# A two-layer encoder in split float32: two products of the up-projection joined into one 512-column matmul, and some weight splits moved to POOL

## The chip, the core and the metric

The kernel runs on one core of a Trainium2 chip. The core has a matrix engine (TensorE, in the rows PE, with its weight loads as PEld), a vector engine (VectorE, DVE), a scalar engine (ScalarE, ACT), a general engine (GpSimd, POOL) and SyncE (SP), which issues the DMA transfers. Engines take their instructions in order and wait for one another by semaphores. Matmuls write to PSUM, which here is cut into eight banks of 128 x 512 float32; everything else lies in SBUF.

The metric is the device time of one execution in microseconds (us). It was 642.43 us before the change: the median of three runs that lay between 642.16 and 642.54.

## The reference

One sequence of 256 positions with 1024 features goes through two layers. Each layer adds the output of two groups of attention heads, and then a gated feed-forward network (FFN) with a short convolution. The FFN is the part that the change touches:

```python
D_FF = 2816
def conv_ffn(h, w_up, conv_w, conv_b, w_down):        # h: rmsnorm(x), 256 x 1024
    u = h @ w_up                                      # 256 x 5632, gate and up columns
    u = conv1d(u, conv_w, width 3, per column) + conv_b
    g, up = jnp.split(u, 2, axis=-1)
    return (jax.nn.silu(g) * up) @ w_down             # 256 x 1024
for l in range(2):
    x = x + attention_groups(rmsnorm(x), ...) @ w_out
    x = x + conv_ffn(rmsnorm(x, ffn_norm[l]), w_up[l], conv_w[l], conv_b[l], w_down[l])
```

All weights and activations are float32.

## The kernel before

A float32 product is made from three products of a faster matmul type (fp32r). Each operand is split into a high part, which is the operand rounded to that type, and a low part, which is what is left; then hi·hi, hi·lo and lo·hi are added up in PSUM. The fourth, lo·lo, is left out. So every product appears three times in the code and in the rows.

**Weights.** The class Weights (L138 to L225) streams all weights through SBUF in one fixed order of units. Raw tiles of 2048 columns come by DMA (`load`, L158); four may be in flight or in use, and a unit of the FFN has 1024 columns, so that a raw tile holds two. For each unit `split_hi` copies the raw columns on ACT into the high part `wh` (L176), and `split_lo` subtracts on DVE raw minus high into the low part `wl` (L189). Six pairs of `wh` and `wl` exist. `fill` issues the next splits, as many as the units already used up by TensorE allow.

**FFN.** The 2816 columns are cut into NF = 22 blocks of 128. Stage j does three things.

- `up(j)` on PE: the gate half and the up half, each with a weight unit of its own. A half takes 8 steps k over the 1024 features, and each step has three products of 128 x 256 columns: high weights with high x (`xh`, L1106), high weights with low x (`xl`, L1107) and low weights with high x (L1108). From j = 2 on both halves lie side by side in one PSUM bank: the bank A for j = 2, then two banks S in turn. The stages 0 and 1 have a bank for each half and are begun before the rest.
- `gate(j)`: DVE multiplies the bank by `r2b`, the RMS scale of each position (one 128x512 product, L284). ACT makes scale and bias of the convolution's middle tap (two Identity copies, L296), four scalar-times-tensor-plus-tensor instructions on DVE add the other taps (L293), ACT does Silu, DVE multiplies the two halves, ACT copies the result to `mh` (high), and DVE subtracts to get `ml` (low). Three times in `gate` a `W.fill(2)` puts weight splits between these steps.
- `down(j-3)` on PE: the 128 rows of the down weights that belong to the block three stages back. For each of four output tiles it adds `mh`·high, `ml`·high and `mh`·low (L1150 to L1152, 128 x 512 each), 12 products into four banks that stay open for the whole layer.

The last four down blocks are held back to the end of the layer, where they are done tile by tile, so that the next layer's norm can begin early. The up weights come from the same stream as the down weights, in the order gate j, up j, down j-3: in layer 0 the units 30+3j, 31+3j and 32+3j.

The order inside one engine is set in two ways. The attention part and the first halves of the stages 0 and 1 are written in program order. The loop over j (L1172 to L1188) is ordered by the language's scheduler, by its own estimates; so the places where weight splits stand among the gate's steps differ from stage to stage, and a change in the loop can move them.

POOL does small work for the attention, and nothing in the FFN.

Of the kernel before, what the change touches and what calls it, by code (L numbers as in the profile page):

```python
# [11 lines left out]
F32R = mybir.dt.float32r  # L12
I32 = mybir.dt.int32
AF = mybir.ActivationFunctionType
ALU = mybir.AluOpType
# [4 lines left out]
P = 128  # L20
LINE = 32
D_MODEL = 1024
SEQ = 256
# [9 lines left out]
NF = D_FF // P  # L33
# [12 lines left out]
FFN_HOLD = 4  # L46
# [91 lines left out]
class Weights:  # L138
# [41 lines left out]
    def split_lo(self):  # L180
        u = self.n_lo
        t, o, last = self.where[u]
        n = self.units[u][-1]
        hi = self.parts[u][0]
        lo = self.w_pool.tile([P, 1024], F32R, name=f"wl{u}", tag="wlo")
        g = self.gain(self.units[u])
        raw, hi = self.raw[t][:, o:o + n], hi.bitcast(F32)[:, :n]
        if g is None:
            self.nc.vector.tensor_tensor(out=lo[:, :n], in0=raw, in1=hi, op=ALU.subtract)  # L189
        else:  # L190
            self.nc.vector.scalar_tensor_tensor(out=lo[:, :n], in0=raw, scalar=g, in1=hi,
                                                op0=ALU.mult, op1=ALU.subtract)
        self.parts[u].append(lo)
        self.n_lo += 1
        if last:
            del self.raw[t]
            self.load()
# [43 lines left out]
def encoder(ctx: ExitStack, tc: tile.TileContext, wpk, x, prm, cst, oh, rb, pos, out):  # L241
# [4 lines left out]
    work = ctx.enter_context(tc.tile_pool(name="work", bufs=2))  # L246
# [5 lines left out]
    def nm(s):  # L252
        uid[0] += 1
        return f"{s}_{uid[0]}"

    def wide():
        return work.tile([P, 512], F32, name=nm("t2"), tag="t2", bufs=7)

    def mid():
        return work.tile([P, 256], F32, name=nm("t1"), tag="t1", bufs=9)  # L260
# [4 lines left out]
    def small(n, dt=F32):  # L265
        return work.tile([P, max(n, LINE)], dt, name=nm("s"), tag=f"s{n}_{dt}", bufs=8 if n <= 32 else 2)[:, :n]
# [4 lines left out]
    def bank():  # L271
        return psa.tile([P, 512], F32, name=nm("S"), tag="S", bufs=2)

    def tbank():
        return psa.tile([P, 512], F32, name=nm("A"), tag="A", bufs=1)

    def obank():
        return psa.tile([P, 512], F32, name=nm("O"), tag="O", bufs=1)

    def acc():  # L280
        return psa.tile([P, 512], F32, name=nm("acc"), tag="acc", bufs=4)

    def tt(o, a, b, op):
        nc.vector.tensor_tensor(out=o, in0=a, in1=b, op=op)  # L284
# [7 lines left out]
    def stt(o, a, s, b, op0, op1):  # L292
        nc.vector.scalar_tensor_tensor(out=o, in0=a, scalar=s, in1=b, op0=op0, op1=op1)  # L293

    def act(o, a, f, **kw):
        nc.scalar.activation(o, a, f, **kw)  # L296
# [15 lines left out]
    mm = nc.tensor.matmul  # L312
# [143 lines left out]

    def new_xT():
        s = State()
        s.hi = work.tile([P, 8, SEQ], F32R, name=nm("xh"), tag="xh", bufs=1)
        s.lo = work.tile([P, 8, SEQ], F32R, name=nm("xl"), tag="xl", bufs=1)  # L460
        s.ss = small(4)
        return s

# [154 lines left out]
    def layer(l, sx, late, bias):  # L618
# [360 lines left out]
        sf = new_xT()  # L979
# [105 lines left out]
        r2b = work.tile([P, SEQ], F32, name=nm("r2b"), tag="r2b", bufs=1)  # L1085

        def ffn_scale():
            xT_stats(sf)
            ob = obank()
            dg = mid()  # L1090
            for t in range(2):
                ts(dg[:, t * P:t * P + P], ident, sf.r[:, t:t + 1], ALU.mult)
            mm(ob[:, :SEQ], ones, dg, start=True, stop=True)
            act(r2b, ob[:, :SEQ], AF.Copy)
# [4 lines left out]
        def up(j, pu, ks=range(8)):  # L1099
            for half in range(2):  # L1100
                u = u_f + FFN_AT[("gate", "up")[half], j]
                hi, lo = W.get(u)
                o = pu[half][:, :SEQ] if len(pu) == 2 else pu[0][:, half * SEQ:(half + 1) * SEQ]
                for k in ks:
                    kp = slice(k * P, k * P + P)
                    mm(o, hi[:, kp], sf.hi[:, k, :], start=k == 0, stop=False)  # L1106
                    mm(o, hi[:, kp], sf.lo[:, k, :], start=False, stop=False)  # L1107
                    mm(o, lo[:, kp], sf.hi[:, k, :], start=False, stop=k == 7)  # L1108
                if ks[-1] == 7:
                    W.done(u)  # L1110

        def gate(j, pu):
            s, y = wide(), wide()
            if len(pu) == 2:
                for g in range(2):
                    tt(s[:, g * SEQ:(g + 1) * SEQ], pu[g][:, :SEQ], r2b, ALU.mult)
            else:
                tt(s.rearrange("p (g t) -> p g t", g=2), pu[0].rearrange("p (g t) -> p g t", g=2),
                   r2b.unsqueeze(1).to_broadcast([P, 2, SEQ]), ALU.mult)
            for g in range(2):  # L1120
                b = j + NF * g
                act(y[:, g * SEQ:(g + 1) * SEQ], s[:, g * SEQ:(g + 1) * SEQ], AF.Identity,
                    scale=cw[:, 44 + b:45 + b], bias=cb[:, b:b + 1])
            W.fill(2)
            for g in range(2):
                b = j + NF * g
                yg, sg = y[:, g * SEQ:(g + 1) * SEQ], s[:, g * SEQ:(g + 1) * SEQ]
                stt(yg[:, 1:], sg[:, :SEQ - 1], cw[:, b:b + 1], yg[:, 1:], ALU.mult, ALU.add)
                stt(yg[:, :SEQ - 1], sg[:, 1:], cw[:, 88 + b:89 + b], yg[:, :SEQ - 1], ALU.mult, ALU.add)
            sl, gt = mid(), mid()  # L1130
            act(sl, y[:, :SEQ], AF.Silu)
            W.fill(2)
            tt(gt, sl, y[:, SEQ:], ALU.mult)
            m = State()
            m.hi = work.tile([P, 1, SEQ], F32R, name=nm("mh"), tag="mh", bufs=6)
            m.lo = work.tile([P, 1, SEQ], F32R, name=nm("ml"), tag="ml", bufs=6)
            act(m.hi[:, 0, :], gt, AF.Copy)
            W.fill(2)
            tt(m.lo[:, 0, :], gt, m.hi.bitcast(F32)[:, 0, :], ALU.subtract)
            gates[j] = m  # L1140
# [13 lines left out]
        def down(j):  # L1154
            for t in range(2):
                for c in range(2):
                    down_mm(j, t, c)
            W.done(u_f + FFN_AT["down", j])
# [13 lines left out]
        for j in range(NF):  # L1172
            if j < 2:
                pu = first[j]
                up(j, pu, range(4, 8))
            else:
                pu = [tbank() if j == 2 else bank()]
                up(j, pu)
            if j == 0:
                continue  # L1180
            if j == 1:
                ffn_scale()
                gate(0, first[0])
            gate(j, pu)
            if j == 1:
                box["a"] = [[acc(), acc()], [acc(), acc()]]
            if FFN_LAG <= j < NF + FFN_LAG - FFN_HOLD:
                down(j - FFN_LAG)  # L1188
# [101 lines left out]
```

## Time and profile before

| | before |
|---|---|
| median of three runs | 642.43 us |
| the profiled execution | 642.16 us |
| its span (first to last instruction) | 640.4 us |
| PE busy | 627.8 us, 98% |
| DVE busy | 497.4 us, 78% |
| ACT busy | 395.8 us, 62% |
| POOL busy | 58.9 us, 9% |
| TensorE clock granted, mean | 0.996 of full speed |

The profiled execution lies 0.27 us under the median, and 1.76 us of it lie outside the span. Busy time of an engine is the union of its instructions. A duration of an instruction runs from its start to its last write; engines overlap the end of one with the start of the next, so that the distance from start to start (the pitch) is shorter than the duration when instructions stand close. The FFN of layer 0 lies between about 134 and 320 us of the span, that of layer 1 between about 446 us and the end.

### The profile page before, as it was taken

What the parts mean: (1) busy time and instruction counts of PE and PEld (TensorE: products, weight loads), DVE (VectorE), ACT (ScalarE), POOL (GpSimd) and SP (SyncE); (2) the same over time, 40 slices, a digit from 0 to 9 for tenths busy, and PEclk for the clock granted to TensorE, in tenths of its full rate; (3) what the DMA queues carried; (4) which work ended last, traced back from release to release, by engine and by line L of the source; (5) the groups of instructions that cost most, each with busy time, mean ns of one, the idle gap of its engine ahead of it and who ended that gap; (6) DMA issues with size and microseconds to landing.
All of it is one profiled execution on the core that took longest, in us unless ns stands there. A gap on an engine that the chain in (4) does not pass through costs nothing.

```text
span 640.4 us, 10656 instructions
## 1 busy us (share of the span) xinstructions
PE 627.8 (98%) x4018; PEld 554.6 (87%) x4018; DVE 497.4 (78%) x1010; ACT 395.8 (62%) x723; POOL 58.9 (9%) x173
## 2 busy tenths in 40 slices
PE   8999999999999999999999999999999999999997
PEld 7967867789999999999899887677999999999995
DVE  4796779679977777777699867876899777777773
ACT  5982867648655555555478557765685555555541
POOL 3950250000000000000001105200000000000000
PEclk8999999999999999999999999999999999999999
DMA  8759425133665455554336512423337445545401
GB/s 314 267 204 174 180 74 198 67 132 139 209 246 180 171 180 193 198 196 152 106 130 262 192 66 75 151 104 133 141 143 278 172 188 197 198 173 170 152 1 66
DMA packets 17706, 105.18 MB, mean 164 GB/s; under 512 B 2102, under 2 KB 3799, under 8 KB 6648
## 3 DMA queue, kind: packets, MB, share of 16 engines
q1 hardware_dynamic: 17368, 104.17, 46.6%
q8 instruction: 31, 0.51, 0.3%
q10 hardware_dynamic: 288, 0.34, 0.2%
q14 instruction: 19, 0.16, 0.1%
HBM read 103.20 MB, written 1.31 MB: 163 GB/s over the span
## 4 chain that ended last, share of the span: by engine, by line
PE 89%; DVE 5%; POOL 3%; issue 1%; ACT 1%; DMA 1%; SPq 0%; DVEq 0%
PE S L1108 12%; PE S L1107 12%; PE S L1106 12%; PE acc L1152 6%; PE acc L1151 6%; PE acc L1150 6%; PE acc L499 4%; PE acc L497 4%; PE acc L498 4%; PE S L558 3%; PE acc L944 2%; PE O L607 2%; PE acc L947 2%; PE acc L946 2%; PE A L535 1%; POOL s L304 1%
## 5 line engine op out<-in xcount | busy, mean ns | idle before, releaser
L176 ACT ACTIVATE wh<-raw 128x1024 fp32r<-128x1024 f32 (+3 forms) x188 | 193.0, 1036 | 96.4 <-PE S L1107 63.5
L189 DVE TENSOR_TENSOR wl<-raw,wh 128x1024 fp32r<-128x1024 f32 (+3 forms) x188 | 223.1, 1190 | 26.6 <-ACT wh L176 26.3
L1108 PE MATMUL S<-xh,wl 128*128 128x256 f32 x640 | 181.0, 283 | 0.0
L1107 PE MATMUL S<-xl,wh 128*128 128x256 f32 x640 | 181.0, 283 | 0.0
L1106 PE MATMUL S<-xh,wh 128*128 128x256 f32 x640 | 180.8, 283 | 0.0
L1107 PEld LDWEIGHTS S<-xl,wh 128*128 128x128 f32 x640 | 122.7, 192 | 1.4
L1106 PEld LDWEIGHTS S<-xh,wh 128*128 128x128 f32 x640 | 122.6, 192 | 1.6
L1108 PEld LDWEIGHTS S<-xh,wl 128*128 128x128 f32 x640 | 122.7, 192 | 0.0
L293 DVE SCALAR_TENSOR_TENSOR t<-t,prm_s,t 128x255 f32<-128x255 f32 x176 | 73.9, 479 | 1.0 <-ACT t L296 0.9
L1152 PE MATMUL acc<-wl,mh 128*128 128x512 f32 x176 | 69.3, 394 | 0.0
L1150 PE MATMUL acc<-wh,mh 128*128 128x512 f32 x176 | 69.3, 394 | 0.0
L1151 PE MATMUL acc<-wh,ml 128*128 128x512 f32 x176 | 69.2, 393 | 0.0
L497 PE MATMUL acc<-wh,xh 128*128 128x512 f32 (+2 forms) x160 | 61.6, 385 | 1.0 <-ACT nat L296 0.9
L499 PE MATMUL acc<-wl,xh 128*128 128x512 f32 (+2 forms) x160 | 58.6, 366 | 0.2 <-DVE wl L189 0.2
L498 PE MATMUL acc<-wh,xl 128*128 128x512 f32 (+2 forms) x160 | 58.3, 364 | 0.2 <-DVE xl L293 0.2
L296 ACT ACTIVATE t<-t,prm_s 128x256 f32<-128x256 f32 x88 | 47.7, 590 | 6.6 <-DVE t L284 6.6
L296 ACT ACTIVATE mh<-t 128x256 fp32r<-128x256 f32 x44 | 18.2, 415 | 46.4 <-DVE t L284 46.4
L284 DVE TENSOR_TENSOR t<-S,r2b 128x512 f32<-128x512 f32 (+1 forms) x42 | 27.9, 665 | 23.0 <-PE S L1108 22.9
L296 ACT ACTIVATE t<-A 96x256 f32<-96x256 f32 (+2 forms) x40 | 18.8, 469 | 43.8 <-PE A L535 26.6
L1152 PEld LDWEIGHTS acc<-wl,mh 128*128 128x128 f32 x176 | 33.1, 188 | 7.5
L1150 PEld LDWEIGHTS acc<-wh,mh 128*128 128x128 f32 x176 | 33.4, 190 | 5.9
L1151 PEld LDWEIGHTS acc<-wh,ml 128*128 128x128 f32 x176 | 33.1, 188 | 6.1
(173 smaller groups left out, 965.0 us busy)
## 6 DMA issues: line engine op xcount, KB each, us to landing
raw<-in_wpk_dram SPq DMA_DIRECT2D x86, 1024.0 KB, 4.8
raw<-in_wpk_dram SPq DMA_DIRECT2D x3, 896.0 KB, 4.4
raw<-in_wpk_dram SPq DMA_DIRECT2D x3, 768.0 KB, 5.6
raw<-in_wpk_dram SPq DMA_DIRECT2D x2, 816.0 KB, 5.2
Bn<-scr SPq DMA_DIRECT2D x8, 192.0 KB, 10.7
raw<-in_wpk_dram SPq DMA_DIRECT2D x2, 720.0 KB, 5.6
X<-in_x_dram SPq DMA_DIRECT2D x3, 256.0 KB, 4.8
raw<-in_wpk_dram SPq DMA_DIRECT2D x2, 384.0 KB, 5.1
```

Of the source, the lines that this page charges most:

```text
L176: self.nc.scalar.activation(hi[:, :n], self.raw[t][:, o:o + n], AF.Copy, scale=1.0 if g is None else g)
L189: self.nc.vector.tensor_tensor(out=lo[:, :n], in0=raw, in1=hi, op=ALU.subtract)
L296: nc.scalar.activation(o, a, f, **kw)
L497: mm(o, lhs.hi[:, k, sl], rh, start=k == 0, stop=False)
L498: mm(o, lhs.lo[:, k, sl], rh, start=False, stop=False)
L499: mm(o, lhs.hi[:, k, sl], rl, start=False, stop=k == ktot - 1)
L1106: mm(o, hi[:, kp], sf.hi[:, k, :], start=k == 0, stop=False)
L1107: mm(o, hi[:, kp], sf.lo[:, k, :], start=False, stop=False)
L1108: mm(o, lo[:, kp], sf.hi[:, k, :], start=False, stop=k == 7)
L1150: mm(o, m.hi[:, 0, sl], hi[:, cs], start=j == 0, stop=False)
L1151: mm(o, m.lo[:, 0, sl], hi[:, cs], start=False, stop=False)
L1152: mm(o, m.hi[:, 0, sl], lo[:, cs], start=False, stop=j == NF - 1)
```

## The change

From stage 2 on, `up` multiplies the high weights with the high and the low x in one matmul of 512 columns. For that, `xh` and `xl` become two halves of one tile (`xhl`). The first 256 columns of the result hold hi·hi and the other 256 hold hi·lo; the product lo·hi still has 256 columns and adds to the first. Since a half now fills a whole bank, each half has a bank of its own: even stages use the banks A and O, odd stages two banks S.

The two column groups must be added before the gate's first step. ACT copies the second group of each half from PSUM to a tile `c`, DVE adds the first group from PSUM and `c`, and the product with `r2b` then has both operands in SBUF.

The low splits of down weights of the blocks 0 to 14 go from DVE to POOL, 15 in each layer. Stages 0 and 1 are computed as before.

```diff
--- before.py
+++ after.py
@@ -186,7 +186,9 @@
         g = self.gain(self.units[u])
         raw, hi = self.raw[t][:, o:o + n], hi.bitcast(F32)[:, :n]
         if g is None:
-            self.nc.vector.tensor_tensor(out=lo[:, :n], in0=raw, in1=hi, op=ALU.subtract)
+            down = self.units[u][1] == "down" and self.units[u][2][0] < NF - FFN_HOLD - 3
+            eng = self.nc.gpsimd if down else self.nc.vector
+            eng.tensor_tensor(out=lo[:, :n], in0=raw, in1=hi, op=ALU.subtract)
         else:
             self.nc.vector.scalar_tensor_tensor(out=lo[:, :n], in0=raw, scalar=g, in1=hi,
                                                 op0=ALU.mult, op1=ALU.subtract)
@@ -456,8 +458,8 @@
 
     def new_xT():
         s = State()
-        s.hi = work.tile([P, 8, SEQ], F32R, name=nm("xh"), tag="xh", bufs=1)
-        s.lo = work.tile([P, 8, SEQ], F32R, name=nm("xl"), tag="xl", bufs=1)
+        s.both = work.tile([P, 2, 8, SEQ], F32R, name=nm("xhl"), tag="xhl", bufs=1)
+        s.hi, s.lo = s.both[:, 0], s.both[:, 1]
         s.ss = small(4)
         return s
 
@@ -1100,22 +1102,31 @@
             for half in range(2):
                 u = u_f + FFN_AT[("gate", "up")[half], j]
                 hi, lo = W.get(u)
-                o = pu[half][:, :SEQ] if len(pu) == 2 else pu[0][:, half * SEQ:(half + 1) * SEQ]
+                o = pu[half]
                 for k in ks:
                     kp = slice(k * P, k * P + P)
-                    mm(o, hi[:, kp], sf.hi[:, k, :], start=k == 0, stop=False)
-                    mm(o, hi[:, kp], sf.lo[:, k, :], start=False, stop=False)
-                    mm(o, lo[:, kp], sf.hi[:, k, :], start=False, stop=k == 7)
+                    if j < 2:
+                        mm(o[:, :SEQ], hi[:, kp], sf.hi[:, k, :], start=k == 0, stop=False)
+                        mm(o[:, :SEQ], hi[:, kp], sf.lo[:, k, :], start=False, stop=False)
+                        mm(o[:, :SEQ], lo[:, kp], sf.hi[:, k, :], start=False, stop=k == 7)
+                        continue
+                    mm(o.rearrange("p (g t) -> p g t", g=2), hi[:, kp], sf.both[:, :, k, :], start=k == 0, stop=False)
+                    mm(o[:, :SEQ], lo[:, kp], sf.hi[:, k, :], start=False, stop=k == 7)
                 if ks[-1] == 7:
                     W.done(u)
 
         def gate(j, pu):
-            s, y = wide(), wide()
-            if len(pu) == 2:
-                for g in range(2):
-                    tt(s[:, g * SEQ:(g + 1) * SEQ], pu[g][:, :SEQ], r2b, ALU.mult)
-            else:
-                tt(s.rearrange("p (g t) -> p g t", g=2), pu[0].rearrange("p (g t) -> p g t", g=2),
+            s, y, c = wide(), wide(), wide() if j >= 2 else None
+            for g in range(2):
+                sg, pg = s[:, g * SEQ:(g + 1) * SEQ], pu[g][:, :SEQ]
+                if j < 2:
+                    tt(sg, pg, r2b, ALU.mult)
+                    continue
+                cg = c[:, g * SEQ:(g + 1) * SEQ]
+                act(cg, pu[g][:, SEQ:], AF.Copy)
+                tt(sg, pg, cg, ALU.add)
+            if j >= 2:
+                tt(s.rearrange("p (g t) -> p g t", g=2), s.rearrange("p (g t) -> p g t", g=2),
                    r2b.unsqueeze(1).to_broadcast([P, 2, SEQ]), ALU.mult)
             for g in range(2):
                 b = j + NF * g
@@ -1174,7 +1185,7 @@
                 pu = first[j]
                 up(j, pu, range(4, 8))
             else:
-                pu = [tbank() if j == 2 else bank()]
+                pu = [bank(), bank()] if j % 2 else [tbank(), obank()]
                 up(j, pu)
             if j == 0:
                 continue
```

In `NF - FFN_HOLD - 3` NF is 22 and FFN_HOLD is 4. `tbank` and `obank` give the banks A and O, `bank` gives the next S, `wide` a 128 x 512 tile of SBUF out of a pool of seven, `act` an ACT instruction and `tt` a two-operand DVE instruction. In the changed kernel L284 becomes L286, L293 becomes L295, L296 becomes L298, and the line of the low split, L189, becomes L191.

The order on TensorE inside a half (`S` is the bank, `wh` and `wl` are high and low weights, `xh` and `xl` the two parts of x) was, for each k:

```order
L1106 MATMUL S_2443<-xh_896,wh_2328 128x256
L1107 MATMUL S_2443<-xl_897,wh_2328 128x256
L1108 MATMUL S_2443<-xh_896,wl_2405 128x256
```

and is now, at the end of one half and the start of the next:

```order
L1113 MATMUL S_2225<-xhl_895,wh_2113 128x512
L1114 MATMUL S_2225<-xhl_895,wl_2187 128x256
L1113 MATMUL S_2226<-xhl_895,wh_2185 128x512
```

Two rows stand where three stood, and the second half goes to another bank.

On DVE, in the middle of an FFN, a stage of before (`t2` are the gate's wide tiles, `t1` its narrow ones, `wl` the low splits, and `x4` means four instructions alike):

```order
L189 TENSOR_TENSOR wl90_3615<-raw47_3354,wh90_3536 128x1024
L284 TENSOR_TENSOR t2_562_3514<-S_561_3465,r2b_406_1783 128x512
L189 TENSOR_TENSOR wl91_3619<-raw47_3354,wh91_3613 128x1024
L293 SCALAR_TENSOR_TENSOR t2_563_3515<-t2_562_3514,prm_s_74,t2_563_3515 128x255 x4
L189 TENSOR_TENSOR wl92_3632<-raw48_3435,wh92_3617 128x1024
L284 TENSOR_TENSOR t1_565_3534<-t1_564_3533,t2_563_3515 128x256
L284 TENSOR_TENSOR ml_567_3544<-t1_565_3534,mh_566_3543 128x256
```

The same on DVE in the changed kernel, around stage 12 of layer 0:

```order
L191 TENSOR_TENSOR wl72_2935<-raw38_2704,wh72_2866 128x1024
L286 TENSOR_TENSOR ml_536_2790<-t1_534_2782,mh_535_2789 128x256
L286 TENSOR_TENSOR t2_539_2839<-A_537_2805,t2_541_2841 128x256
L191 TENSOR_TENSOR wl73_2939<-raw38_2704,wh73_2933 128x1024
L286 TENSOR_TENSOR t2_539_2839<-O_538_2806,t2_541_2841 128x256
L286 TENSOR_TENSOR t2_539_2839<-t2_539_2839,r2b_404_1781 128x512
L295 SCALAR_TENSOR_TENSOR t2_540_2840<-t2_539_2839,prm_s_74,t2_540_2840 128x255 x4
L286 TENSOR_TENSOR t1_543_2864<-t1_542_2863,t2_540_2840 128x256
L191 TENSOR_TENSOR wl75_3017<-raw39_2775,wh75_2950 128x1024
```

Before, splits stood between the product with `r2b`, the four taps and the product of the halves; now none stands there, and the two that remain stand with the adds ahead of the product. The third, wl74, stands on POOL.

At the start of the FFN of layer 0, DVE had after the scale of the norm:

```order
L189 TENSOR_TENSOR wl40_1970<-raw22_1645,wh40_1962 128x1024
L189 TENSOR_TENSOR wl41_2055<-raw22_1645,wh41_1968 128x1024
L189 TENSOR_TENSOR wl42_2061<-raw23_1726,wh42_2053 128x1024
L284 TENSOR_TENSOR t2_433_1943<-acc_407_1784,r2b_406_1783 128x256
L284 TENSOR_TENSOR t2_433_1943<-acc_408_1785,r2b_406_1783 128x256
```

and has now (`ml_436` is the low part of the gate of stage 0):

```order
L191 TENSOR_TENSOR wl40_1968<-raw22_1643,wh40_1960 128x1024
L191 TENSOR_TENSOR wl42_2049<-raw23_1724,wh42_2041 128x1024
L286 TENSOR_TENSOR t2_431_1941<-acc_405_1782,r2b_404_1781 128x256
L286 TENSOR_TENSOR t2_431_1941<-acc_406_1783,r2b_404_1781 128x256
L286 TENSOR_TENSOR t2_437_1975<-S_407_1784,r2b_404_1781 128x256
L286 TENSOR_TENSOR t2_437_1975<-S_408_1785,r2b_404_1781 128x256
L295 SCALAR_TENSOR_TENSOR t2_432_1942<-t2_431_1941,prm_s_74,t2_432_1942 128x255 x4
L295 SCALAR_TENSOR_TENSOR t2_438_1976<-t2_437_1975,prm_s_74,t2_438_1976 128x255 x4
L286 TENSOR_TENSOR t2_449_2031<-A_447_1997,t2_451_2033 128x256
L286 TENSOR_TENSOR t1_434_1958<-t1_433_1957,t2_432_1942 128x256
L286 TENSOR_TENSOR t2_449_2031<-O_448_1998,t2_451_2033 128x256
L191 TENSOR_TENSOR wl43_2109<-raw23_1724,wh43_2047 128x1024
```

with `ml_436` behind the last row. The split wl41 has gone from here; it is the first of POOL's, which has nothing between them:

```order
L191 TENSOR_TENSOR wl41_2043<-raw22_1643,wh41_1966 128x1024
L191 TENSOR_TENSOR wl44_2115<-raw24_1776,wh44_2107 128x1024
L191 TENSOR_TENSOR wl47_2204<-raw25_1964,wh47_2191 128x1024
L191 TENSOR_TENSOR wl50_2288<-raw27_2111,wh50_2273 128x1024
L191 TENSOR_TENSOR wl53_2370<-raw28_2189,wh53_2357 128x1024
```

These are five of the 15 of layer 0; the rest follow every third unit up to wl83.

## Rows read from the trace of the kernel before

**Rows 1.** Page, parts 1 and 4: busy time by engine; chain that ended last, by engine

```profile
PE 627.8 (98%) x4018; PEld 554.6 (87%) x4018; DVE 497.4 (78%) x1010; ACT 395.8 (62%) x723; POOL 58.9 (9%) x173
...
PE 89%; DVE 5%; POOL 3%; issue 1%; ACT 1%; DMA 1%; SPq 0%; DVEq 0%
```

**Rows 2.** Stretch 170 to 303: PE, PEld, DVE, ACT, POOL busy, clock, DMA, GB/s

```profile
170.00:303.00 133.00, 133.00 (x941) 125.07 (x940) 104.90 (x160) 75.48 (x111) 0.00 (x0) 1.00 0.55 191
```

**Rows 3.** Timeline of PE, layer 0: start us, duration us, engine, line, output<-inputs, tiles

```profile
179.39 0.28 PE L1106 MATMUL S<-xh,wh 128*128 128x256 f32 x1
...
185.14 0.39 PE L1150 MATMUL acc<-wh,mh 128*128 128x512 f32 x1
...
187.92 0.28 PE L1106 MATMUL S<-xh,wh 128*128 128x256 f32 x1
```

**Rows 4.** Timeline of DVE and POOL in the attention parts

```profile
33.55 0.18 DVE L706 CUSTOM_DVE_ANT_0 t<-krs 128x32 f32<-128x32 f32 x1
33.64 0.32 POOL L299 TENSOR_TENSOR s<-krs,cosg 128x64 f32<-128x64 f32 x1 [0.64 <-DVE s L284]
...
33.66 0.36 DVE L706 CUSTOM_DVE_ANT_0 t<-krs 128x32 f32<-128x32 f32 x1
...
77.62 0.22 POOL L299 TENSOR_TENSOR s<-s,s 128x16 f32<-128x16 f32 x1
...
78.21 1.21 DVE L189 TENSOR_TENSOR wl<-raw,wh 128x1024 fp32r<-128x1024 f32 x1
78.22 1.27 POOL L299 TENSOR_TENSOR s<-s,s 128x16 f32<-128x16 f32 x1
```

**Rows 5.** Groups of POOL by shape: busy us, mean ns of one, idle before

```profile
L299 POOL TENSOR_TENSOR nat<-nat,fd 128x512 f32<-128x512 f32 x4 | 4.1, 1045 | 0.2
...
L299 POOL TENSOR_TENSOR s<-s 128x16 f32<-128x16 f32 x12 | 2.6, 216 | 12.7 <-DVE s L290 12.1
```

**Rows 6.** Timeline of POOL, at the kernel's start

```profile
13.01 0.25 POOL L299 TENSOR_TENSOR s<-s,s 128x32 f32<-128x32 f32 x1
```

**Rows 7.** Timeline of DVE, layer 0, a stage without gaps

```profile
161.14 0.69 DVE L284 TENSOR_TENSOR t<-S,r2b 128x512 f32<-128x512 f32 x1
161.74 0.42 DVE L284 TENSOR_TENSOR t<-t,t 128x256 f32<-128x256 f32 x1
162.07 1.22 DVE L189 TENSOR_TENSOR wl<-raw,wh 128x1024 fp32r<-128x1024 f32 x1
163.21 0.42 DVE L284 TENSOR_TENSOR ml<-t,mh 128x256 fp32r<-128x256 f32 x1
163.54 1.67 DVE L293 SCALAR_TENSOR_TENSOR t<-t,prm_s,t 128x255 f32<-128x255 f32 x4
165.12 1.22 DVE L189 TENSOR_TENSOR wl<-raw,wh 128x1024 fp32r<-128x1024 f32 x1
...
169.20 0.69 DVE L284 TENSOR_TENSOR t<-S,r2b 128x512 f32<-128x512 f32 x1
```

**Rows 8.** Timeline of DVE, ACT and PE at the FFN's start, layer 0

```profile
148.49 3.50 DVE L189 TENSOR_TENSOR wl<-raw,wh 128x1024 fp32r<-128x1024 f32 x3
...
150.28 0.36 ACT L296 ACTIVATE r2b<-O 128x256 f32<-128x256 f32 x1
...
159.56 0.39 PE L1150 MATMUL acc<-wh,mh 128*128 128x512 f32 x1
```

**Rows 9.** Timeline of PE and DVE at the last stage of layer 0

```profile
313.04 0.39 PE L1150 MATMUL acc<-wh,mh 128*128 128x512 f32 x1
...
313.24 0.69 DVE L284 TENSOR_TENSOR t<-S,r2b 128x512 f32<-128x512 f32 x1 [1.82 <-PE S L1108]
...
314.60 1.92 DVE L293 SCALAR_TENSOR_TENSOR t<-t,prm_s,t 128x255 f32<-128x255 f32 x4 [0.21 <-ACT t L296]
316.63 0.42 DVE L284 TENSOR_TENSOR t<-t,t 128x256 f32<-128x256 f32 x1
317.54 0.43 DVE L284 TENSOR_TENSOR ml<-t,mh 128x256 fp32r<-128x256 f32 x1 [0.48 <-ACT mh L296]
```

## The prediction

> **What bounds the kernel now.** I read the busy times first: PE works in 98% of the span, and 89% of the chain that ended last is PE [rows 1]. Then I looked for waits inside an FFN: in the 133 us of the middle of layer 0, PE has no gap and its clock is at its upper level of 2.4 GHz (granted 1.00); DVE is busy for 79%, ACT for 57%, the DMA engines for 55% [rows 2]. So a microsecond less of matmul is a microsecond less of time, as long as no engine that feeds PE becomes slower than PE. The one to watch is DVE.
>
> **PE, the gain.** From 179.39 to 185.14 lie the 48 products of an `up`: 5.75/48 = .1198 us each. From 185.14 to 187.92 lie the 12 products of a `down`: 2.78/12 = .2317, or .2312 over longer stretches [rows 3]. A `down` product has 512 columns. The joined product takes the place of two of .1198 and costs .2312 if its two runs of 256 columns stream like one of 512: .0084 us saved. With 16 in a stage, 20 stages, two layers: 640 x .0084 = 5.4 us. A stage goes from 8.53 us (5.75 + 2.78) to 8.395. What the joined product mainly saves is an instruction, not columns, so the gain is small beside the work it gives to others.
>
> **ACT.** It gets two copies of 256 columns from PSUM in a stage; such a copy takes .36 [rows 8]. Its load in the 16 stages of rows 2 rises from 57% to some 66%: hidden, as far as its place in the chain below is not the last.
>
> **The banks.** Stage 2 now needs the bank O, which `r2b` occupies: its copy ends at 150.28 + .36 = 150.64 [rows 8], and PE, by the pitches of rows 3 from the row at 159.56 back, reaches the second half of stage 2 some .3 us later. Nothing. Afterwards the bank of stage j is wanted again by stage j+2, 11.2 us after `up(j)` ended (8.395 + 2.78): a DVE that lags by less stops nobody.
>
> **DVE, outside POOL.** Pitches from a stage without gaps [rows 7]: the product with r2b .60 (161.14 to 161.74), a 256-column instruction .33 (161.74 to 162.07), a split 1.14 (162.07 to 163.21), or 1.22 to its last write, four taps 1.58. This stage made up for lag: with four splits and four 256-column instructions it is .60 + 4.56 + 1.58 + 1.32 = 8.06, and rows 7 have 169.20 - 161.14 = 8.06, so the pitches add up. A usual stage has three splits and two 256-column instructions, .60 + 3.42 + 1.58 + .66 = 6.26; now two splits and, with the adds, four: .60 + 2.28 + 1.58 + 1.32 = 5.78. Without POOL, DVE gets .48 us of room in a stage.
>
> **POOL and DVE exclude each other.** This is the costly term. A 128x16 product on POOL takes .22 at 77.62; the same beside a split on DVE (78.21 to 79.42) takes 1.27 and ends when the split has ended. The other way round, a DVE instruction of .18 takes .36 while a POOL product runs [rows 4]. So an instruction of either that reads two operands in SBUF stops the other's. The split on POOL is of this kind, and so are the taps, the splits on DVE, the product of the halves, `ml`, and now the product with r2b, which read PSUM before. The two adds read PSUM and one tile, and no row shows whether such an instruction is stopped.
>
> The Trainium skill ("SBUF — State Buffer", "Who interferes with whom") states the same as a lock held for a whole instruction, and that a DVE instruction with at most one SBUF input doesn't contend. Rows 4 agree with the first (1.27 against .22); the second no row here shows. By it the adds run beside POOL, and the sum below changes by nothing, since an add lies there beside the split anyway.
>
> How long is a split on POOL (D)? No row has 1024 columns. A 128x512 product takes 1.045, a 128x16 product .216 [rows 5]: the line through both gives 1.90 at 1024, and doubling the first 2.09. With two different operand tiles it may be dearer (128x32 at .25 [rows 6] is .03 over 128x16 for 16 columns: 1.9 ns a column, to which a start of .19 adds 2.1). I take D = 2.2, a little above the nearest row doubled, since the write is of another type and beside the traffic of DMA; bounds 1.9 and 2.5. Below nothing: if it falls only into DVE's idle time.
>
> The Trainium skill ("GPSIMD Engine Reference", "3.1 Elementwise — side-by-side cycle accounting") gives 4497 ns for a float32 add of 2048 columns; half of it would be an estimate of 2.25, against 2.09 from the row above doubled. By it the sum below would come out 30 x .05 = 1.5 us later than at 2.2.
>
> **The chain on DVE with POOL in it.** In the new order no split stands between the product with r2b and the product of the halves, so nothing fills ACT's part there: that distance is 316.63 - 313.24 = 3.39 (ACT's two Identity copies, the taps, Silu in series) [rows 9]. Behind it stand the product of the halves .33, a split 1.14, `ml` .33, an add .33, a split 1.22, and then POOL's split D (the second add beside it), before the next product with r2b. That is 6.74 + D for a stage. Against PE's 8.395 it breaks even at D = 1.65; at 2.2 it is 8.94. POOL's split stands there because ACT makes its high part only behind those of the two others.
>
> In layer 0, POOL begins wl41 when wl40 has ended, 148.49 + 1.22 = 149.71 [rows 8]. Then come two POOL splits (wl41, wl44), a split 1.14, four 256-column products 1.32, eight taps 3.16, three adds and products .99, a split 1.22, and two of 256 columns .66: the product of stage 2 is at 158.20 + 2D. From there to that of stage 15 it takes 5.78 + 6.19 + 11 x 6.74 = 86.11 and 13 D (the first two stages start with splits already made, 6.19 being 3.39 + 1.14 + 5 x .33). The last six stages have no split on POOL: 6.99 (3.39 + 2.28 + 1.32), two of 5.78, two of 8.06 with four splits, and 5.50 with two splits of 384 columns (.43 each, by their columns) for one whole: 40.17. Stage 21's product is thus at 284.48 + 15 D.
>
> When is it due? The last `up` of before ends at 313.04, and without stalls now 20 x .135 earlier, at 310.34. After it PE has nine tiles of three `down` products (.695 each), 6.26, and one product more, .23, before it needs the low part of stage 21, which is ready 4.73 after the product (317.97 - 313.24) [rows 9]. So the product is due by 312.1. The delay is 15 D - 27.6: 5.4 us at D = 2.2. In layer 1, where the splits of 384 columns are missing, .86 less: 4.5.
>
> The first place where this shows is `down(0)`: its second product needs the low part of stage 0, which now comes at 157.96 + 2D = 162.4 at D = 2.2, and PE is there at 159.5 (159.56 + .23, less two stages' gain) [rows 8]. That stall of 2.9 us is a part of the 5.4, not added to it; but where D is so small that the end costs nothing, it remains, 2.2 us a layer at D = 1.9.
>
> **The sum.** 5.4 gained, 5.4 + 4.5 = 9.9 lost: 4.5 us slower than the profiled execution's 642.16, which is 646.7. The median shown lies .27 above that execution, less than can be told. At D = 1.9 only the start stalls remain: -5.4 + 4.5 = -.9, 641.3. At 2.09: delays 3.75 and 2.85, +1.2, 643.4. At 2.5: 9.9 and 9.0, +13.5, 655.7.
>
> **Rivals.**
>
> - *The gain stays.* POOL's splits fall mostly where DVE waits for ACT: the gap between the product with r2b and the product of the halves has 3.39 - .60 - 1.58 - .33 = .9 us without DVE work, and if POOL comes later than the product by that, the taps are held only for D - .9. A stage is then near 6.2 + D, 8.4 at 2.2, and PE is not passed. For it: DVE's and POOL's work without gaps is 5.78 + 2.2 = 7.98, under 8.395. Against it: the order puts POOL ahead of the product once DVE lags. The time is 642.16 - 5.4 = 636.8 with no stall at all, and up to 641.1 with the stalls at the start; some 638.5.
> - *Even.* D is 1.9 to 2.05 and the gain pays the start: 641.1 to 643.4.
> - *The joined product brings nothing.* Its moving operand has two runs of 256 columns, 2048 apart; if the jump costs more than the .0084 us saved, PE gains nothing or loses. No row shows two runs of that size. With no gain and the delays, less what a slower PE takes up of them, the time is some 646 to 652. This one is slower than before even if POOL costs nothing, from .01 us a product on.
> - *Beyond.* D of 2.5 and more, or POOL and DVE handing over with a pause: over 655.
>
> **The numbers.** Slower by POOL in DVE's chain, 643.4 to 655.7, has a chance of .43; the gain stays .36; even .13; the joined product brings nothing .05; beyond .03. The forecast is the first, 646.7. My range of 637 to 655 takes in the gain that stays and leaves some 2 in 10; the forecast's own is 643.4 to 655. A difference of 0.2% (1.3 us) is about what a measurement of this kernel tells from none. Faster by more has .36, none .13, slower .43 + .05 + .03 = .51.
>
> **What would show it.** Right, if POOL's split takes 2.1 to 2.3, products with r2b in stages 5 to 14 stand 8.9 apart, DVE's taps and splits are longer beside POOL, PE waits 2 to 3 us at the second product of `down(0)` and again for the low part of the last stage, in both layers, and the joined product has a pitch of .231. Wrong, if PE has no gap but the one at `down(0)`, or if POOL's split runs beside the taps without lengthening either; and the gain's size is wrong if the joined product's pitch is .24 or more.

## The result, and the profile after

The changed kernel takes 649.28 us (median of four runs, 648.24 to 650.25), against 642.48 us before. The ratio is 1.0107, with a 95% interval from 1.0093 to 1.0121: slower by 6.8 us. The profiled execution took 649.81 us, its span is 648.0.

The page's first part, and the two longest waits of PE, which the kernel before doesn't have; the columns of the second fence are what PE waited with and for, us in total, times, and the longest:

```profile
PE 626.6 (97%) x3378; PEld 520.1 (80%) x3378; DVE 544.5 (84%) x1060; ACT 415.2 (64%) x803; POOL 137.1 (21%) x203
```

```profile
PE acc L1162 <- DVE ml L286: 4.1, 2, 2.1
PE acc L1161 <- ACT mh L298: 3.6, 3, 1.6
```

PE waits for the gate's low part twice, once in each layer, and for its high part at the layers' ends. These are the two places that the prediction named, only that it had expected the low part at the end too. In layer 0 the first wait and the longest one at the end are these:

```profile
163.54 0.50 PE L1162 MATMUL acc<-wh,ml 128*128 128x512 f32 x1 [2.00 <-DVE ml L286]
...
323.79 0.50 PE L1161 MATMUL acc<-wh,mh 128*128 128x512 f32 x1 [1.65 <-ACT mh L298]
```

What POOL does to DVE shows in one stage of the middle of layer 0, to be read against [rows 7]. First DVE, then POOL:

```profile
230.88 2.45 DVE L286 TENSOR_TENSOR t<-t,r2b 128x512 f32<-128x512 f32 x1
234.00 1.92 DVE L295 SCALAR_TENSOR_TENSOR t<-t,prm_s,t 128x255 f32<-128x255 f32 x4 [0.67 <-ACT t L298]
236.02 0.43 DVE L286 TENSOR_TENSOR t<-t,t 128x256 f32<-128x256 f32 x1
236.50 1.23 DVE L191 TENSOR_TENSOR wl<-raw,wh 128x1024 fp32r<-128x1024 f32 x1
237.64 0.42 DVE L286 TENSOR_TENSOR ml<-t,mh 128x256 fp32r<-128x256 f32 x1
237.98 0.42 DVE L286 TENSOR_TENSOR t<-S,t 128x256 f32<-128x256 f32 x1
238.31 1.21 DVE L191 TENSOR_TENSOR wl<-raw,wh 128x1024 fp32r<-128x1024 f32 x1
239.44 0.41 DVE L286 TENSOR_TENSOR t<-S,t 128x256 f32<-128x256 f32 x1
239.89 2.44 DVE L286 TENSOR_TENSOR t<-t,r2b 128x512 f32<-128x512 f32 x1
```

```profile
230.28 2.50 POOL L191 TENSOR_TENSOR wl<-raw,wh 128x1024 fp32r<-128x1024 f32 x1 [6.51 <-ACT wh L176]
239.29 2.49 POOL L191 TENSOR_TENSOR wl<-raw,wh 128x1024 fp32r<-128x1024 f32 x1 [6.51 <-ACT wh L176]
```

The product with r2b took .69 in [rows 7] and takes 2.44 here; it ends .55 after POOL's split has ended (239.29 + 2.49 = 241.78, 242.33). The add that reads a bank S starts at 239.44, inside POOL's split, and takes its .41. From product to product it is 239.89 - 230.88 = 9.01 us, and it is 9.0 to 9.1 in eleven intervals of layer 0 in a row.

PE meanwhile keeps a steady pace. The start of an `up` and the first row of the `down` after it, against [rows 3]:

```profile
241.71 0.40 PE L1113 MATMUL S<-xhl,wh 128*128 128x512 f32 x1
241.94 0.28 PE L1114 MATMUL S<-xhl,wl 128*128 128x256 f32 x1
242.06 0.39 PE L1113 MATMUL S<-xhl,wh 128*128 128x512 f32 x1
...
247.26 0.39 PE L1161 MATMUL acc<-wh,mh 128*128 128x512 f32 x1
```

That is 5.55 us for an odd stage instead of 5.75 (an even one, from 250.04 to 255.68, takes 5.64).

**Where the 7.6 us between the spans come from**, by the starts of `up` and `down` in both traces. In layer 0, from the first `up` to the last product, it was 324.82 - 134.13 = 190.69 and is 329.64 - 135.42 = 194.22: +3.5. In layer 1 it was 189.82 and is 193.14: +3.3. Ahead of layer 0 it is 1.3 more. At 20 us of the span only .1 of it is there, and at 39 us all of it (ACT's load of a table starts at 37.94 before and at 39.20 now), so it arises in the attention of the first layer. The other kernels' profiled runs, most of them with the same attention code, reach the FFN within .3 of the kernel before, so I put it down to that run and not to the change, though no run was made for it. What follows the last product of layer 1 makes up the rest: 4.3 us instead of 4.8, -.5.

### The profile page after: what moved, and what is told of

Same layout as the page of the kernel before. It is cut to its first block, busy times and chain, and to the rows that moved or that the text cites. A ratio compares the mean times of both kernels' runs of the same rounds, so it can differ in the third digit from the quotient of the medians.

```text
span 648.0 us, 9572 instructions
## 1 busy us (share of the span) xinstructions
PE 626.6 (97%) x3378; PEld 520.1 (80%) x3378; DVE 544.5 (84%) x1060; ACT 415.2 (64%) x803; POOL 137.1 (21%) x203
## 4 chain that ended last, share of the span: by engine, by line
PE 78%; DVE 11%; POOL 5%; issue 4%; ACT 1%; DVEq 0%; ACTq 0%; POOLq 0%
PE S L1113 9%; PE acc L1162 6%; PE acc L1161 6%; PE acc L1163 6%; PE A L1113 6%; PE O L1113 5%; PE S L1114 5%; PE acc L499 4%; PE acc L501 4%; PE acc L500 4%; DVE wl L191 3%; PE S L560 3%; PE A L1114 3%; PE O L1114 3%; PE acc L946 2%
## 5 line engine op out<-in xcount | busy, mean ns | idle before, releaser
L191 DVE TENSOR_TENSOR wl<-raw,wh 128x1024 fp32r<-128x1024 f32 (+3 forms) x158 | 189.2, 1199 | 5.7 <-ACT wh L176 4.4
L191 POOL TENSOR_TENSOR wl<-raw,wh 128x1024 fp32r<-128x1024 f32 x30 | 78.4, 2612 | 184.8 <-ACT wh L176 171.8
L1113 PE MATMUL S<-xhl,wh 128*128 128x512 f32 x320 | 112.2, 392 | 0.3 <-DVE t L286 0.2
L298 ACT ACTIVATE t<-t,prm_s 128x256 f32<-128x256 f32 x88 | 47.9, 594 | 85.4 <-DVE t L286 85.3
L295 DVE SCALAR_TENSOR_TENSOR t<-t,prm_s,t 128x255 f32<-128x255 f32 x176 | 82.6, 505 | 19.3 <-ACT t L298 17.4
L1114 PE MATMUL S<-xhl,wl 128*128 128x256 f32 x320 | 89.5, 280 | 0.0
L1113 PEld LDWEIGHTS S<-xhl,wh 128*128 128x128 f32 x320 | 59.9, 187 | 14.4 <-DVE t L286 0.9
L286 DVE TENSOR_TENSOR t<-t,r2b 128x512 f32<-128x512 f32 x40 | 66.6, 1665 | 1.2
L499 PE MATMUL acc<-wh,xhl 128*128 128x512 f32 (+2 forms) x160 | 61.2, 383 | 1.8 <-ACT nat L298 0.9
L1114 PEld LDWEIGHTS S<-xhl,wl 128*128 128x128 f32 x320 | 60.4, 189 | 0.9
L501 PE MATMUL acc<-wl,xhl 128*128 128x512 f32 (+2 forms) x160 | 58.1, 363 | 0.7 <-DVE wl L191 0.7
L500 PE MATMUL acc<-wh,xhl 128*128 128x512 f32 (+2 forms) x160 | 57.9, 362 | 0.2 <-DVE xhl L295 0.2
L1113 PE MATMUL A<-xhl,wh 128*128 128x512 f32 x160 | 58.0, 402 | 0.0
L1113 PE MATMUL O<-xhl,wh 128*128 128x512 f32 x160 | 57.4, 399 | 0.0
L298 ACT ACTIVATE t<-A 128x256 f32<-128x256 f32 (+2 forms) x60 | 26.0, 433 | 43.8 <-PE A L537 26.7
```

The lines of the kernel that those rows point to most:

```text
L191: eng.tensor_tensor(out=lo[:, :n], in0=raw, in1=hi, op=ALU.subtract)
L499: mm(o, lhs.hi[:, k, sl], rh, start=k == 0, stop=False)
L500: mm(o, lhs.lo[:, k, sl], rh, start=False, stop=False)
L501: mm(o, lhs.hi[:, k, sl], rl, start=False, stop=k == ktot - 1)
L1113: mm(o.rearrange("p (g t) -> p g t", g=2), hi[:, kp], sf.both[:, :, k, :], start=k == 0, stop=False)
L1114: mm(o[:, :SEQ], lo[:, kp], sf.hi[:, k, :], start=False, stop=k == 7)
```

## The experiments

The theory throughout: an instruction on POOL that reads two operands in SBUF holds DVE's instructions of that kind; so POOL's split lies in DVE's chain, the chain becomes longer than PE's stage, and the lag is paid at the layer's end. The rivals are in the expectations.

**All splits on DVE.**

```diff
-            down = self.units[u][1] == "down" and self.units[u][2][0] < NF - FFN_HOLD - 3
-            eng = self.nc.gpsimd if down else self.nc.vector
-            eng.tensor_tensor(
+            self.nc.vector.tensor_tensor(
```

> The changed kernel with all low splits back on DVE: joined products, copies and adds stay. Theory (POOL's split holds DVE ahead of the product with r2b, and only that costs): PE keeps its gain of 40 x .135 = 5.4 us and waits for nobody in an FFN, so 642.5 - 5.4 = 637.1, between 636.3 and 638.2; products with r2b stand 8.4 apart, at PE's pace. Rival A (the added copies and adds make the chain of ACT and DVE too long, with POOL or without): still over 643. Rival B (the joined product gains nothing): 642 to 643.

636.67 us, ratio .9915 (.9900 to .9930): 5.8 us faster than before, 12.6 faster than the changed kernel. The page's first part:

```profile
PE 622.2 (98%) x3378; PEld 519.6 (82%) x3378; DVE 521.7 (82%) x1090; ACT 419.8 (66%) x803; POOL 58.8 (9%) x173
```

No wait of PE inside an FFN is left beyond those of before. So the joined product brings what it should, the copies and adds are hidden, and rivals A and B fall. This version beats both kernels. One thing changes along with the engine: the scheduler orders DVE anew and puts a split between the product with r2b and the taps again. So this run alone can't tell the hold from the order; the runs under "The hold by itself" can, as they keep the order.

**POOL's splits alone**, with nothing joined (`before` with the lines marked - in the diff above in place of its own).

> The kernel before, with only the down splits 0 to 14 moved to POOL; nothing is joined. Theory: the splits that stay on DVE lie in the gaps where DVE waits for ACT, the product with r2b reads PSUM and is not held, and DVE's work with POOL's is 6.26 - 1.14 + 2.27 = 7.4 of 8.53 us, so no lag builds up in the middle; what can show is a wait at the first down of a layer. 642 to 645. Rival C (a split on POOL costs its 2.3 us wherever it stands): about 12 us over the before without its split's relief, 650 or more.

642.86 us, ratio 1.0006 (.9997 to 1.0015): no difference. Where DVE meets POOL now, first DVE and then POOL:

```profile
217.07 1.22 DVE L191 TENSOR_TENSOR wl<-raw,wh 128x1024 fp32r<-128x1024 f32 x1
218.21 3.82 DVE L295 SCALAR_TENSOR_TENSOR t<-t,prm_s,t 128x255 f32<-128x255 f32 x4
```

```profile
219.32 2.42 POOL L191 TENSOR_TENSOR wl<-raw,wh 128x1024 fp32r<-128x1024 f32 x1 [6.23 <-ACT wh L176]
```

The four taps take 3.82 instead of 1.67, so POOL holds DVE here too. The expectation had no lag in the middle, by a sum of 7.4; the chain came out longer, as DVE also waits twice in a stage for ACT's high parts (.48 and .53 us). But a stage takes 8.65, only .12 over PE's 8.53, and that lag is made up before the layer's end, in stages of 7.45; the layers are .5 and .4 us longer, all of it from ahead of the first `down`. So POOL's split is not costly by itself; it costs where DVE has no room for it.

**POOL's split behind the product.** A 128x1 product on POOL, into the first column of the tile that the split then fills, makes POOL wait:

```diff
...
+            if down and self.mark is not None:
+                self.nc.gpsimd.tensor_tensor(out=lo[:, :1], in0=self.mark[:, :1], in1=self.mark[:, :1], op=ALU.mult)
             eng.tensor_tensor(out=lo[:, :n], in0=raw, in1=hi, op=ALU.subtract)
...
+            W.mark = s if j < NF - 1 else None
```

`mark` is the tile `s` of the last gate.

> The changed kernel, in which POOL begins a down split only when the product with r2b of the last gate is done (a 128x1 product on POOL reads that gate's tile first); the same number of splits on POOL and DVE's order nearly unchanged. Theory (place decides): POOL's 2.3 us begin where DVE waits for ACT's Identity copies, of which some .75 us hide, and the second add is not beside it any more: 3.39 + 1.55 + 3.68 = 8.6 us a stage instead of 9.01, lag at the layer's end falls by some 4 us a layer, and the stall at the first down stays: 640 to 643. Rival C (the lock costs the same wherever it stands): 648 to 651.

658.05 us, ratio 1.0235 (1.0218 to 1.0252): where I expected it to be faster than the changed kernel, it is slower. First DVE, then POOL, in a stage of the middle:

```profile
214.13 0.69 DVE L289 TENSOR_TENSOR t<-t,r2b 128x512 f32<-128x512 f32 x1
215.56 3.80 DVE L298 SCALAR_TENSOR_TENSOR t<-t,prm_s,t 128x255 f32<-128x255 f32 x4 [0.74 <-ACT t L301]
```

```profile
214.97 0.20 POOL L193 TENSOR_TENSOR wl<-t 128x1 fp32r<-128x1 f32 x1 [6.53 <-PE acc L1167]
215.24 2.41 POOL L194 TENSOR_TENSOR wl<-raw,wh 128x1024 fp32r<-128x1024 f32 x1
```

The product is free again (.69), and the taps take the hold: 3.80 instead of 1.92. (The row of the small product names PE as what it waited for. PE's last product ends at 214.84 and the product with r2b at 214.13 + .69 = 214.82, and the rows one stage earlier and one later name DVE.) Of POOL's 2.41 only .32 fell into DVE's wait for ACT (215.24 to 215.56), since the small product and its semaphore came first, and the second add, which ran beside POOL before, now stands outside. From product to product it is 9.20 (223.34 - 214.13 is 9.21). Nothing was won by this place, as DVE idles there for .74 us and POOL takes 2.41. Here rival C, 648 to 651, came nearer to the truth than my sum, but neither reaches 658. The time is 8.8 us over the changed kernel's. In layer 0, which is 5.6 us longer, 1.9 have arisen by the product of stage 5, 2.1 come from the longer intervals up to stage 21, and the rest at the layer's end. PE's waits have places that the changed kernel hardly has: 6.4 us for banks that DVE has not read yet (.2 there) and 3.0 us for low weights. This was not taken apart further.

**POOL from block 4 on.** The condition for POOL becomes `4 <= block < NF - FFN_HOLD - 3`.

> The changed kernel with POOL's splits only for the down blocks 4 to 14, so that none stands at an FFN's start. Theory (one DVE chain through the layer, each POOL split costs 2.27 and each DVE split 1.14): no wait at the first down, and the end delay of some 6.1 us a layer falls by 4 x 1.13 = 4.5, to 1.6: 637.1 + 3.2 = 640.3, between 638.5 and 642. Rival D (only the start counts, as DVE has slack later): 637. Rival E (only the lag at the end counts and the start's stall is separate from it): 646 or more, by the waits of the end that stay.

641.30 us, ratio .9983 (.9965 to 1.0001), within the theory's range and far from rival D's 637 and rival E's 646. The profiled execution was the shortest of ten, 639.68. No wait for a low part is left at the first `down`; in the middle the products again stand 9.01 apart; and at the layers' ends stays

```profile
PE acc L1161 <- ACT mh L298: 2.6, 2, 1.6
```

which is less than the 3.6 above. Over the version with all splits on DVE, layer 0 is 2.1 us longer and layer 1 1.5 (by the starts of the first `up`, or of its last part, and the last product): 3.6, where the chain gave 3.2. So start and end are one chain, which rival E denied.

**Every other block on POOL** (`... and block % 2 == 1`).

> The changed kernel with POOL making only the low splits of the odd down blocks up to 13 (7 of 15 in a layer); the others are on DVE. Theory (a chain on DVE that must not pass PE's pace, added up over neighbouring stages): a stage with a POOL split takes up to 9.0, one without 6.9 to 7.9, so two together stay at or under 16.8, PE's pace for two, and no lag is left at the layer's end; only one POOL split lies in the start, and the low part of stage 0 comes about as PE reaches it. 636.7 to 639. Rival C (every POOL split costs PE its share of the loss, 12.6 us / 30 = .42 each): 14 x .42 = 5.9 over 636.7, that is 642.6.

639.36 us, ratio .9958 (.9944 to .9973): 2.7 us over the version with all on DVE, less than half of rival C's 5.9, and .4 above the theory's range. The layers' ends show no wait; the whole difference is at the first `down` of each layer:

```profile
PE acc L1162 <- DVE ml L286: 2.9, 2, 1.5
```

The theory's middle is right: intervals of 6.16 and 10.58 make 16.74 for two stages, and that is PE's own pace (6.83 and 9.94, 16.77, with all splits on DVE). Its start was not: one POOL split there costs some 1.5 us a layer, which I had put at about nothing.

**The hold by itself.** A control (all splits on DVE, pools of gate tiles smaller to make room for a scratch tile) and two kernels whose order on PE, DVE and ACT is that of the control. In one POOL makes the 30 splits again into a tile that nobody reads; in the other it writes that tile twice with a constant, behind a 128x1 product that makes it wait.

```diff
...
+            if self.units[u][1] == "down" and self.units[u][2][0] < NF - FFN_HOLD - 3:
+                scr = self.w_pool.tile([P, 1024], F32, name=f"scr{u}", tag="scr", bufs=1)
+                self.nc.gpsimd.tensor_tensor(out=scr[:, :n], in0=raw, in1=hi, op=ALU.subtract)
+            self.nc.vector.tensor_tensor(out=lo[:, :n], in0=raw, in1=hi, op=ALU.subtract)
...
```

```diff
...
+                self.nc.gpsimd.tensor_tensor(out=scr[:, :1], in0=hi[:, :1], in1=hi[:, :1], op=ALU.mult)
+                self.nc.gpsimd.memset(scr[:, :n], 0.0)
+                self.nc.gpsimd.memset(scr[:, :n], 1.0)
...
```

> Control for the next two: the joined products with all low splits on DVE, and two pools of gate tiles smaller (t2 from 7 to 6 buffers, t1 from 9 to 7) to make room for a scratch tile; the order of the instructions is the same as with the larger pools. Both theories: 636.7, as that kernel, if the buffers are enough; up to 638 if a gate waits for one.

> The control, and POOL makes in addition each of the 30 low splits of the down blocks 0 to 14 into a scratch tile that nobody reads. DVE makes the real ones; the orders of PE, DVE and ACT are those of the control. Theory (POOL's instruction holds DVE's two-operand instructions): DVE's work of 6.92 a stage and POOL's 2.27 exclude each other, 9.2 a stage against PE's 8.395; products with r2b stand about 9.2 apart in stages 4 to 15, lag .8 x 11 = 9 us a layer and the start's two holds of 2.3, less the slack at the end: 650 to 660. Rival F (it was the hand-over, POOL's result coming late to PE, and not a hold on DVE): nobody waits for the scratch tile, so 636.7 to 638 as the control.

> The control, and POOL writes the scratch tile twice with a constant (128x1024 each) at each of the same 30 places, after a 128x1 product that makes it wait for the high part. It reads no SBUF in these. Theory (what excludes is that both read): DVE's taps and splits keep their .48 and 1.22 beside it, and the time is the control's, 636.7 to 638. Rival G (any POOL instruction on SBUF holds DVE): longer by what two memsets take, some 2 us in each of 26 stages: 645 or more.

The control took 636.71 us (ratio .9906, .9886 to .9925). With the unused splits it is 662.42 (1.0316, 1.0273 to 1.0359), 25.7 us more, which is also over the theory's 660, though nobody waits for their result; the products with r2b stand 8.13 and 10.37 apart in turn, 9.25 on average, where the theory gave 9.2. Nor does the trace show an engine or a transfer's issue that waits for these splits to have read their inputs. With the constants it is 636.18 (.9898, .9878 to .9917), as the control. The unused split, first DVE and then POOL:

```profile
225.05 1.22 DVE L192 TENSOR_TENSOR wl<-raw,wh 128x1024 fp32r<-128x1024 f32 x1
226.19 3.85 DVE L296 SCALAR_TENSOR_TENSOR t<-t,prm_s,t 128x255 f32<-128x255 f32 x4
```

```profile
227.34 2.41 POOL L191 TENSOR_TENSOR scr<-raw,wh 128x1024 f32<-128x1024 f32 x1 [8.92 <-ACT wh L176]
```

and the constants, at about the same place:

```profile
222.98 1.67 DVE L298 SCALAR_TENSOR_TENSOR t<-t,prm_s,t 128x255 f32<-128x255 f32 x4
224.71 1.22 DVE L194 TENSOR_TENSOR wl<-raw,wh 128x1024 fp32r<-128x1024 f32 x1
```

```profile
223.18 0.95 POOL L192 MEMSET scr<- 128x1024 f32 x1
224.19 0.96 POOL L193 MEMSET scr<- 128x1024 f32 x1
```

The taps go from 1.67 to 3.85 beside the subtract and stay at 1.67 beside the writes. So the loss is a hold on DVE, not POOL's result coming late (rival F) and not POOL's being busy (rival G). The Trainium skill ("SBUF — State Buffer", "Who interferes with whom") says just this of a DVE instruction with two inputs in SBUF: it contends with a GpSimd instruction that reads SBUF, not with one that only writes it. The 3.85 beside the subtract and the 1.67 and 1.22 beside the writes agree.

**Without copies and adds**, POOL's splits kept:

```diff
...
-                act(cg, pu[g][:, SEQ:], AF.Copy)
-                tt(sg, pg, cg, ALU.add)
...
+                tt(sg, pg, r2b, ALU.mult)
...
```

> The changed kernel with POOL's splits, but without the copies and adds: the second 256 columns (hi x lo) are computed and left out of the result, and the products with r2b read PSUM, one for each half, as in stages 0 and 1. Theory (what POOL holds is the product, whose operands now lie in SBUF, and nothing fills ACT's gap): the product is not held, DVE's work with POOL's is .66 + 2.28 + 1.58 + .66 + 2.27 = 7.45 a stage, so little lag: 637 to 641, with a wait at the first down. Rival C (POOL's split costs its 2.3 us wherever it falls, the taps held instead): a stage near 8.7 as with POOL alone, lag .3 x 11 and the start: 641 to 645. Rival A (the copies and adds are no part of the loss): 648 or more.

641.03 us, ratio .9977 (.9967 to .9988): where the theory's range ends and rival C's begins. The products with r2b read PSUM and take .42; POOL holds the product of the halves instead, DVE and then POOL:

```profile
228.43 2.50 DVE L286 TENSOR_TENSOR t<-t,t 128x256 f32<-128x256 f32 x1
```

```profile
228.25 2.40 POOL L191 TENSOR_TENSOR wl<-raw,wh 128x1024 fp32r<-128x1024 f32 x1 [6.17 <-ACT wh L176]
```

A stage takes 8.55, .15 over PE's, and not 7.45 as the theory summed: the hold falls on another instruction, as rival C says, and DVE waits for ACT besides (.48 and .19 us). So the copies, the adds and the product from SBUF, which went together here, are part of the loss: they make DVE's stage .46 longer, 9.01 instead of 8.55. But without POOL they cost nothing, as the first experiment has it.

## Why the prediction was right, step by step

- **The forecast.** 646.7, slower, with 643.4 to 655 as its own range; 649.28 came. It was the case named first that came in, by its mechanism and at its places. The time alone would not show that, as the rival in which the joined product brings nothing has 646 to 652; the experiments do.
- **The gain on PE.** 5.4 forecast. The joined product with its partner takes (5.55 + 5.645)/32 = .350 a step, where .351 was worked out from [rows 3], and the version without POOL's splits is 5.8 faster. So the joined product brings its gain, and the rival without one is out.
- **POOL's split.** D = 2.2 was the term that was too small. Rows have 2.49, of which some .2 run beside the end of DVE's split before it; what DVE loses is 9.01 - 6.74 = 2.27. Read directly, from the end of DVE's split (238.31 + 1.21 = 239.52) to the end of POOL's (241.78), it is 2.26. The doubled 128x512 row (2.09) was the near one, the line (1.90) too low. The Trainium skill's figure for 2048 columns ("GPSIMD Engine Reference", "3.1 Elementwise — side-by-side cycle accounting") halves to an estimate of 2.25, nearer to 2.27 than my value; the rows' own 2.49 in the middle, and 2.39 for the shortest of 30, are longer than it.
- **The chain.** 6.74 + D is right: with 2.27 put in, the product of stage 2 is due at 162.7 and came at 163.74, less the 1.3 that this run started late, 162.4; and the delays 15 D - 27.6 and 15 D - 28.5 become 6.45 and 5.6. Against the version with all on DVE, layer 0 is 6.3 us longer and layer 1 6.1. Inside a stage two deviations that nobody foresaw cancel: from POOL's end to the product of the halves it is 3.24 instead of 3.39 (232.78 to 236.02), and behind that product .48 pass instead of .33, as the split there waits for ACT's high part (235.42 + 1.04 = 236.46; the split starts at 236.50).
- **The sum.** The .07 too little in D is 30 x .07 = 2.1 us; with it the forecast would have been 4.5 + 2.1 = 6.6 over, against 6.8. That it comes so near is in part luck: the gain is .4 larger than forecast and the loss, 12.6 by the first experiment instead of 12.05, larger by about as much, and the four runs of the changed kernel lie 2 us apart.
- **The wait at the first `down`.** 2.9 forecast; the `down` went from 2.78 to 5.06 us, so 2.3 came, in layer 0. PE itself reached it some .6 later than forecast. In layer 1 that `down` takes 6.48, 3.7 more; what is beyond the wait is TensorE's clock (below).
- **The adds beside POOL.** They are let through (239.44, .41), which was taken as a case that changes nothing.
- **The signs.** The pitch of the joined product, .23, and the two places of PE's waits came as said. Three did not quite: POOL's split has 2.49 in the rows instead of 2.1 to 2.3, the products stand 9.0 apart instead of 8.9, and DVE's taps and splits in the middle are not longer (1.92 and 1.21 to 1.23). What POOL holds there is the product with r2b, the place that the chain of the prediction gave it.
- **"The gain stays".** This rival, POOL falling into DVE's gap, got .36. It failed as said against it: the order puts POOL ahead of the product. In the experiment that forced POOL behind the product it failed as well: POOL's split began .42 after the product's end, and only .32 us of it fell into DVE's gap. A split that begins right at the product's end was not tried.

## What to carry to other kernels

Moving an elementwise instruction from DVE to POOL gave DVE no time in this kernel, where both read two operands in SBUF: it takes 2.27 us of DVE's time here and gives back 1.14. Ask first for the length of the slower engine's chain with the moved instruction in it, not for the sum of busy times: DVE and POOL together had 5.78 + 2.27 = 8.05 of 8.395 us, and the chain had 9.0. And where a change frees one engine and loads another, try its halves apart: the half that was to help DVE cost all that the other gained, and more.

## What had not been expected

Within the FFNs TensorE's clock fell once, behind the stall at the first `down` of layer 1. In the windows below the columns are the length, PE, PEld, DVE, ACT and POOL busy, granted clock, DMA share and GB/s:

```profile
476.00:478.00 2.00, 0.49 (x3) 0.17 (x1) 2.00 (x2) 0.61 (x1) 2.00 (x1) 1.00 0.40 82
478.00:480.00 2.00, 1.43 (x5) 1.17 (x6) 2.00 (x5) 1.11 (x2) 0.24 (x1) 0.91 0.96 401
480.00:482.00 2.00, 2.00 (x6) 1.61 (x5) 2.00 (x3) 1.77 (x5) 0.00 (x0) 0.50 0.14 45
482.00:484.00 2.00, 2.00 (x9) 1.63 (x9) 2.00 (x6) 1.37 (x2) 0.42 (x1) 0.74 0.84 274
```

PE idles for 2.1 us, goes on at the upper level of 2.4 GHz (granted 1.00 from 478 to 479), and falls to 1.2 GHz (.50 from 480 to 482) for some 3 us in all, in which a `down` product has a pitch of .43 instead of .23: about 1.6 us. A stall of 2.0 us in layer 0 left the clock alone (granted 1.00 from 155 to 169). The loss doesn't show in the time: against the version with all splits on DVE, layer 1 is 6.1 us longer and layer 0, without it, 6.3. I take it that DVE's lag at the layer's end hides it; no run was made for that.

With the joined product, the `up` of a stage takes 5.65 and 5.55 us in turn; before, each took 5.75. It is not the banks: in the changed kernel those with A and O take 5.65 and those with two banks S 5.55, and with all splits on DVE it is the other way round. What makes the difference was not tried.
